# A hybrid decoder trunk on one core: semaphore waits in the scheduler's model, and a lead-in written anew

## The chip, the cores and the metric

The kernel runs on one core of one Trainium2 chip. The metric is the time of one execution on the device in microseconds (us); the median of three runs is given, and beside it one execution that the hardware profiler recorded. Five engines work in parallel, each on its own instruction stream in order: TensorE (PE; its weight loads are listed apart as PEld), VectorE (DVE), ScalarE (ACT), GpSimd (POOL) and SyncE (SP), which issues all transfers here. They wait for each other through semaphores.

## The reference, cut to what matters

Two layers over 1024 positions of 1024 channels in float32, then one RMSNorm. What the change touches is the beginning of the first layer:

```python
def rms_norm(x, g):
    y = x32 * lax.rsqrt(jnp.mean(x32 * x32, axis=-1, keepdims=True) + NORM_EPS)
    return (y * g).astype(x.dtype)

def hybrid_layer(x, c_act, positions, norm_g, w_ada, b_ada, w_in, ...):
    mod = c_act @ w_ada + b_ada
    shift, scale, gate = jnp.split(mod[:, None, :], 3, axis=-1)
    h = rms_norm(x, norm_g) * (1.0 + scale) + shift
    proj = h @ w_in
    ...  # three mixers: windowed pooling, chunked retention, RWKV-7 time mixing
    y = jnp.einsum('btnw,nwd->btnd', branches, w_branch)
    merged = jnp.sum(sigmoid(gate_logits) * y, axis=2)
    return x + gate * (merged @ w_out)

c_act = jax.nn.silu(c)
for l in range(DEPTH):          # DEPTH = 2
    x = hybrid_layer(x, c_act, positions, ...)
return rms_norm(x, final_g)
```

The vector `c_act` has 1024 values and `w_ada` 3072 columns per layer. Nothing can be multiplied by `w_in` before the sum of squares over all channels is known, and slice by slice of channels only when that slice's shift and scale are.

## The kernel before, in words

The activations are held transposed: channels on the 128 partitions, positions along the free dimension. x comes as 16 tiles of 128 x 512: eight slices of channels (kt 0 to 7) in two halves of the sequence (h 0 and 1). Each product of the big projections is made three times in a reduced-precision format (fp32r): an operand is split into a rounded part (`hhi`, or `wh` and the first part of `wbig` for weights) and the rest (`hlo`, `wl`), and hi*hi, hi*lo and lo*hi are added up in PSUM. One such 128x512 matmul is the unit of TensorE's work.

The Python program records all operations first (class `Prog`), and `weave` then sets the order on every engine: it simulates the engines with a table of durations, takes at each step the engine that can start first, and on it the ready operation of the lowest priority number (the recorder's clock, then the order of writing). `give` replays that order; so almost every instruction stands at one line, L500, and is told by its tiles. Waits follow from the data: where an instruction waits for more than one semaphore, the further ones become instructions of their own ahead of it.

The lead-in of layer 0 is written out by hand in the order of `steps`, `sq`, `normed`, `mms` and their like. Its parts:

- `xdma`, `aload`, `wdma`: transfers of x, of the conditioning weights (`wada`, `ringG`) and of the first three weight tiles (`wr`), in that order on SP. At most eight are outstanding.
- `sq`, `sqadd`, `sums`: ACT squares the eight tiles of a half, DVE (and POOL) adds them up, PE sums over the partitions with four 128x1 matmuls against `ones`.
- `rstd`, `rstd_bc`, `rstd_copy`: square root (`rn`), reciprocal, and a broadcast over the partitions by PE (`rbc`), with a copy in SBUF (`rbs`) for POOL.
- `ada`: the conditioning, in groups. Groups 0 to 3 give shift and scale of kt 0 to 3, group 4 of kt 4 and 5, group 5 of kt 6 and 7. Per group DVE takes eight steps "weight tile times c plus the running sum" (`ada_ps`, the last writes `ada_acc`): 256 columns wide in groups 0 to 3, 512 in 4 and 5. Then PE sums over the partitions (`adaps`) and DVE makes `mod` and `acoef`.
- `normed` (x times rbc), `affine` (ACT: `hhi` and x in two passes), `low` (`hlo`), `wsp` (splits the weights: ACT and POOL), `mms`: for one slice and one half nine matmuls, three weight tiles (lora, k, r) by three products. 8 slices x 2 halves x 9 = 144 matmuls.

In the kernel before, `normed` runs on POOL for kt 4 and 5 of both halves and kt 6 and 7 of half 0, and `low` on POOL for kt 1 to 5. After the lead-in a planner (`plan_layer`) feeds the wide matmuls of the projections to PE, and the mixers' small matmuls (the recurrence's `cy`, `ch` above all) are put between them.

Of the kernel before, what the change touches and what calls it, by code (L numbers as in the profile page):

```python
# [9 lines left out]
F32 = mybir.dt.float32  # L10
# [197 lines left out]
class Op:  # L208
    __slots__ = ("eng", "what", "args", "kw", "outs", "ins", "prio", "lane", "pred", "succ", "n", "i",
                 "dur", "occ", "load", "twice", "lock", "est", "start", "end", "left", "table", "acc")  # L210
# [44 lines left out]
SPACE_LAT = {"PE": 54, "DVE": 34, "ACT": 34, "POOL": 70, "SP": 28}  # L255
SETS = {"Sqrt": 1, "Sin": 2, "Tanh": 3, "Exp": 3, "Sigmoid": 3}


class Prog:
# [143 lines left out]
    def weave(self):  # L403
        ops = self.ops
        for o in ops:
            self.cost(o)
            o.est, o.left = 0.0, len(o.pred)
# [6 lines left out]
        landed, table, pe = [0.0] * 8, 0, [0.0, 0.0]  # L414
        order = []
        other = {"DVE": "POOL", "POOL": "DVE"}
        while len(order) < len(ops):
            best = None
            for e, q in ready.items():
                if not q:  # L420
                    continue
                f = free[e]
                if e == "SP":
                    f = max(f, landed[-8])
                elif e == "PE":
                    f = max(pe[0], pe[1] - 107)
                lk = lock[other[e]] - 100 if e in other else 0.0
# [12 lines left out]
            if e == "PE":  # L440
                m = max(pe[1], max(pe[0], o.est) + o.load)
                if o.twice:
                    m += max(o.load, c)
# [10 lines left out]
            order.append(o)  # L454
            for i in o.succ:
                p = ops[i]
                kind = p.pred[o.i]
                if p.eng != e or e == "SP":
                    r = o.end + SPACE_LAT[p.eng]
                elif kind == "d" and e != "PE":  # L460
                    r = o.end + SPACE_LAT[e]
                else:
                    r = s
                p.est = max(p.est, r)
                p.left -= 1
# [38 lines left out]
def trunk_kernel(ctx, tc, xT, cvec, pos, vecs, consts, w_ada, w_all, pool_w, lora_w, out):  # L504
# [1024 lines left out]
    ring = deque()  # L1529
# [31 lines left out]
    def sums(h, *kts):  # L1561
        ssp[h] = acc_ps()
# [88 lines left out]
    def astep(g, nxt=None):  # L1651
        for _ in range(8):
            steps(gs[g], 1)
            if nxt is not None:
                aload(nxt, 1)

# [18 lines left out]
    steps(gs[0], 4)  # L1675
    rstd_bc(0)
    sq(1, 0, 1)
    sqadd(G_, 1, 0, 1)
    steps(gs[0], 4)
    aload(3, 2)  # L1680
    steps(gs[0], 1)
    rstd_copy(0)
    normed(0, 0)
    sq(1, 2, 3)
    sqadd(G_, 1, 2, 3)
    steps(gs[0], 1)
    sq(1, 4, 5)
    sqadd(G_, 1, 4, 5)
    sq(1, 6, 7)
    normed(0, 1)  # L1690
    sqadd(V, 1, 0, 2)
    ss1 = sums(1, 0, 4)
    next(ss1)
    sqadd(V, 1, 6, 7)
    derive(0)
    sqadd(V, 1, 4, 6)
    next(ss1)
    wsp(0, 0)
    affine(0, 0)
    wsp(0, 1, 2)  # L1700
# [4 lines left out]
    steps(gs[1], 3)
    wdma(1, 0, 1, 2)
    aload(4, 6)
    run(ss1)
    acc6[0] = [acc_ps() for _ in range(3)]
    mms(0, 0)  # L1710
    steps(gs[1], 1)
    rstd_bc(1)
    normed(0, 2, 3)
    steps(gs[1], 1)
    normed(0, 4, eng=G_)
    affine(0, 1)
    low(G_, 0, 1)
    steps(gs[2], 2)
    normed(1, 0)
    affine(1, 0)  # L1720
    steps(gs[2], 1)
    normed(1, 1)
    affine(1, 1)
    low(V, 1, 0)
    normed(1, 2, 3)
# [4 lines left out]
    mms(1, 0)  # L1730
    steps(gs[2], 5)
    normed(0, 5, eng=G_)
    steps(gs[2], 1)
    mms(1, 1)
    steps(gs[3], 2)
    steps(gs[2], 1)
    both(2)
    wsp(1, 0)
    normed(1, 4, eng=G_)
    steps(gs[3], 6)  # L1740
    aload(4, 2)
    mms(0, 2)
    steps(gs[3], 1)
    mms(1, 2)
    steps(gs[4], 2)
    steps(gs[3], 1)
    both(3)
    wsp(1, 1, 2)
    normed(1, 5, eng=G_)
    aload(5, 2)  # L1750
    for _ in range(6):
        steps(gs[4], 1)
        aload(5, 1)
    mms(0, 3)
    steps(gs[4], 1)
    mms(1, 3)
    steps(gs[5], 2)
    steps(gs[4], 1)
    both(4)
    both(5)  # L1760
    normed(0, 6, eng=G_)
    normed(0, 7, eng=G_)
    steps(gs[5], 6)
    normed(1, 6, 7, eng=V)
# [327 lines left out]
```

## Time and profile before

| | |
|---|---|
| median of three runs | 2348.25 us (2347.0 to 2361.45) |
| the profiled execution's own time | 2348.31 us |
| its span, first to last instruction | 2346.2 us |
| PE busy | 2302.1 us, 98% |
| DVE, ACT, POOL busy | 1420.2, 859.1, 841.5 us |

The profile lists instructions with start and duration in us from the span's start. A row of a timeline ends, in brackets, with the idle time before it and what ended that; a row of stretches gives the busy time of each engine, then the clock that PE was granted (1.00 or 0.50), the share of the DMA engines and the rate in GB/s. Matmuls are pipelined: a duration overlaps the next one's, and the distance between starts is the cost.

### The profile page before, as it was taken

The numbers are of one execution on the slowest core, as the hardware profiler recorded it, in microseconds if no ns is written. First come the engines' busy times: TensorE is split into PE (matmuls) and PEld (weight loads), VectorE is DVE, ScalarE is ACT, GpSimd is POOL, SyncE is SP. The second block draws the span as 40 slices with busy tenths as digits, with TensorE's granted clock in tenths as the row PEclk, the third lists the DMA queues.
The fourth block names the chain that finished last, engine by engine and source line by source line (L and its number), as shares of the span: only waits on it lengthen the run. The fifth ranks groups of instructions, "written<-read, shape, count | busy, mean of one in ns | idle before, by whom it ended". The sixth has DMA issues, their size and how long they took to land.

```text
span 2346.2 us, 33803 instructions
## 1 busy us (share of the span) xinstructions
PE 2302.1 (98%) x12520; PEld 1905.3 (81%) x12520; DVE 1420.2 (61%) x2802; ACT 859.1 (37%) x1706; POOL 841.5 (36%) x738
## 2 busy tenths in 40 slices
PE   5999999999999999999999999999999999999998
PEld 4888888888888887788888888888788888888888
DVE  7666478467557744468546746855864784412444
ACT  5633342433333333213443334334433423322343
POOL 5222233233242434463442232323323243246541
PEclk9999999999999999999999999999999999999999
DMA  8132112112213315677431211211221131465442
GB/s 280 41 104 77 41 46 87 41 37 69 73 54 91 102 57 175 208 221 235 155 101 52 73 41 41 91 37 39 80 64 38 58 105 53 131 170 157 131 144 81
DMA packets 126516, 227.78 MB, mean 97 GB/s; under 512 B 14352, under 2 KB 17680, under 8 KB 126352
## 3 DMA queue, kind: packets, MB, share of 16 engines
q1 hardware_dynamic: 126352, 225.63, 31.1%
q8 instruction: 98, 1.61, 0.3%
q14 instruction: 66, 0.54, 0.1%
HBM read 176.56 MB, written 49.02 MB: 96 GB/s over the span
## 4 chain that ended last, share of the span: by engine, by line
PE 92%; DVE 4%; DMA 2%; issue 1%; POOL 1%; ACT 1%; SPq 0%; DVEq 0%; ACTq 0%; POOLq 0%
PE acc L500 76%; PE cy L500 4%; PE ch L500 2%; PE g L500 2%; PE m L500 1%; DMA wada<-in_w_ada 1%; PE ro L500 1%; PE bt L500 1%; PE rkv L500 1%; PE rs L500 1%; PE lw L500 1%; DVE ada_acc L500 1%; PE pps L500 0%; SPq L500 0%; DVE ada_ps L500 0%
## 5 line engine op out<-in xcount | busy, mean ns | idle before, releaser
L500 PE MATMUL acc<-hhi,wh 128*128 128x512 f32 x2000 | 806.4, 403 | 0.4 <-DVE r L500 0.4
L500 PE MATMUL acc<-hhi,wl 128*128 128x512 f32 x2000 | 804.7, 402 | 0.0
L500 PE MATMUL acc<-hlo,wh 128*128 128x512 f32 x2000 | 804.4, 402 | 0.0
L500 POOL TENSOR_TENSOR wl<-wr,wh 128x512 fp32r<-128x512 f32 x342 | 455.5, 1332 | 969.2 <-ACT wh L500 938.9
L500 ACT CAST wh<-wr 128x512 fp32r<-128x512 f32 x342 | 212.1, 620 | 618.5 <-PE acc L500 437.2
L500 PEld LDWEIGHTS acc<-hhi,wh 128*128 128x128 f32 x2000 | 377.0, 189 | 66.8 <-issue 1.5
L500 PEld LDWEIGHTS acc<-hhi,wl 128*128 128x128 f32 x2000 | 377.0, 188 | 66.4 <-issue 1.8
L500 PEld LDWEIGHTS acc<-hlo,wh 128*128 128x128 f32 x2000 | 377.1, 189 | 66.0 <-issue 2.2
L500 PE MATMUL acc<-oG,wh 128*128 128x512 f32 x384 | 150.2, 393 | 2.8 <-ACT oG L500 1.5
L500 PE MATMUL acc<-olo,wh 128*128 128x512 f32 x384 | 150.7, 394 | 1.1 <-POOL olo L500 1.0
L500 PE MATMUL acc<-oG,wl 128*128 128x512 f32 x384 | 150.0, 392 | 0.0
L500 ACT COPY xst<-Z 64x64 f32<-64x64 f32 x256 | 62.5, 244 | 168.3 <-DVE Z L500 165.1
L500 DVE SCALAR_TENSOR_TENSOR S<-ch,pc,SP 64x64 f32<-64x64 f32 x224 | 63.3, 283 | 92.0 <-PE ch L500 86.6
L500 DVE COPY xst<-cy 64x64 f32<-64x64 f32 x256 | 55.4, 216 | 86.8 <-PE cy L500 63.1
L500 DVE TENSOR_TENSOR tm<-VB 64x30 f32<-64x30 f32 (+14 forms) x240 | 101.8, 424 | 7.4
L500 DVE TENSOR_TENSOR VB<-VB,tm 64x30 f32<-64x30 f32 (+14 forms) x240 | 99.4, 414 | 7.4
L500 DVE COPY Z<-ch 64x128 f32<-64x128 f32 x128 | 36.0, 281 | 101.4 <-PE ch L500 101.0
L500 PEld LDWEIGHTS acc<-oG,wh 128*128 128x128 f32 x384 | 72.1, 189 | 19.7 <-ACT oG L500 3.2
L500 PEld LDWEIGHTS acc<-olo,wh 128*128 128x128 f32 x384 | 72.6, 189 | 18.3 <-POOL olo L500 3.5
L500 PEld LDWEIGHTS acc<-oG,wl 128*128 128x128 f32 x384 | 72.5, 189 | 14.8
L500 ACT ACTIVATE gsg<-acc 128x512 f32<-128x512 f32 x88 | 52.4, 596 | 84.9 <-PE acc L500 66.5
L500 DVE SCALAR_TENSOR_TENSOR ada_acc<-wada,cact,ada_acc 128x512 f32<-128x512 f32 (+1 forms) x70 | 64.8, 925 | 26.5 <-DMA wada<-in_w_ada 25.6
(269 smaller groups left out, 3688.3 us busy)
## 6 DMA issues: line engine op xcount, KB each, us to landing
wr<-in_w_all SPq DMA_DIRECT2D x364, 256.0 KB, 2.7
gd<-gsg SPq DMA_DIRECT2D x88, 256.0 KB, 2.0
gs<-gd SPq DMA_DIRECT2D x88, 256.0 KB, 2.8
wada<-in_w_ada SPq DMA_DIRECT2D x70, 256.0 KB, 3.6
ol<-od SPq DMA_DIRECT2D x64, 256.0 KB, 2.9
ringG<-in_w_ada SPq DMA_DIRECT2D x26, 256.0 KB, 4.9
x<-in_xT SPq DMA_DIRECT2D x16, 256.0 KB, 5.0
od<-po SPq DMA_DIRECT2D x16, 256.0 KB, 2.1
```

What stands on the lines that cost most here:

```text
L500: f(*[put(x) for x in o.args], **{k: put(x) for k, x in o.kw.items()})
```

## The change

Two things change. First, `weave` gets another model: an operation that waits for new counts of several semaphores starts 140 ns later on PE, and 70 ns after the earlier ones on DVE, ACT and POOL; PE may be chosen 60 instead of 107 ns ahead; and in the first 60 us PE runs at half speed in a window of 3413 ns that follows one with less than 78% of work.

```diff
-                    f = max(pe[0], pe[1] - 107)
+                    f = max(pe[0], pe[1] - 60)
...
-                m = max(pe[1], max(pe[0], o.est) + o.load)
+                k = int(s / WINDOW) if s < WARM_UP else -1
+                slow = 2 if k == 0 or k > 0 and work[k - 1] < 0.78 * WINDOW else 1
+                ld, c = o.load * slow, c * slow
+                m = max(pe[1], max(pe[0], o.est) + ld)
...
-                o.start, o.end = m, m + d
+                o.start, o.end = m, m + d + c - o.occ
...
+                    new = sorted((k for k, (r, n) in p.arr.items() if n > q.get(k, 0)), key=lambda k: SEMS.get(k, 0))
+                    late = max((r for r, n in p.arr.values()), default=0.0)
+                    if len(new) > 1:
+                        if p.eng == "PE":
+                            late += 140
+                        elif p.eng != "SP":
+                            late = max(late, 70 + max(p.arr[k][0] for k in new[:-1]))
+                    p.est = max(p.est, late)
```

Second, the lead-in of layer 0 is written in another order, and two sums move to PE. `ada_both` replaces `ada` for its six groups: in groups 0 to 3 every second weight tile is multiplied on PE (the tile as stationary operand, a column of c moving, 128x1), the others on DVE as before; groups 4 and 5 stay on DVE. The squares of half 0 are no longer added up on DVE: PE sums all eight (32 matmuls instead of 4). Those of half 1 are added in four pairs, all on DVE (16 matmuls instead of 8). `normed` and `low` run on DVE throughout. The second half of x is loaded behind the conditioning weights, and the weight tiles ahead of most of them.

```diff
+    def ada_both(g):
...
+        mine = [i for i in range(2 * n) if i % 2 == 0 and g < 4]
+        kts = [(i, o) for i in range(2 * n) if i not in mine for o in range(per)]
+        for j, (i, o) in enumerate(kts):
...
+                nc.vector.scalar_tensor_tensor(acc if j == len(kts) - 1 else part, w, c, part, op0=ALU.mult, op1=ALU.add)
...
+        todo += [(acc[:, m * P : (m + 1) * P], ones, m) for m in range(n)]
+        for j, (w, c, m) in enumerate(todo):
+            mmul(ps[:, m : m + 1], w, c, start=j == 0, stop=j == len(todo) - 1, skip_group_check=True)
+        ada_end(0, g, ps)
...
-    aload(0, 4)
+    aload(4)
+    wdma(0, 0, 1, 2)
+    aload(10)
     xdma(1, *range(8))
-    wdma(0, 0, 1, 2)
...
-        if kt:
-            sqadd(V, 0, 0, kt)
-    run(sums(0, 0))
+    run(sums(0, *range(8)))
     rstd(0)
...
+    ada_both(0)
...
+    normed(0, 0)
+    affine(0, 0)
...
+    mms(0, 0)
     normed(0, 1)
+    ada_both(1)
...
+    for kt in range(4):
+        normed(1, kt)
+        affine(1, kt)
+        low(V, 1, kt)
+        mms(1, kt)
+    wsp(1, 0, 1, 2)
+    normed(0, 4, 5, 6, 7)
+    normed(1, 4, 5, 6, 7)
+    ada_both(4)
...
+    both(4, V)
+    both(5, V)
     mms(0, 4)
     mms(1, 4)
```

How this moves the instructions is shown at three places. On PE, at the start of the program, before (acc and ssp are PSUM tiles; `fixed` holds `ones`):

```order
L500 MATMUL acc_151<-fixed,sq_103 128x1 x4
L500 MATMUL rbc_179<-cst,rn_164 128x128 x4
L500 MATMUL adaps_192<-fixed,ada_acc_186 128x1 x2
L500 MATMUL acc_242<-fixed,sq_175 128x1 x4
L500 MATMUL acc_253<-hhi_233,wbig_229 128x512 x2
```

and now:

```order
L526 MATMUL ssp_115<-fixed,sq_137 128x1 x4
L526 MATMUL ssp_115<-fixed,sq_143 128x1 x4
L526 MATMUL adaps_202<-cact,ringG_119 128x1 x8
L526 MATMUL adaps_202<-fixed,ada_acc_179 128x1 x2
L526 MATMUL rbc_227<-cst,rn_208 128x128 x4
L526 MATMUL adaps_241<-cact,ringG_119 128x1 x8
L526 MATMUL adaps_241<-fixed,ada_acc_237 128x1
L526 MATMUL acc_265<-hhi_253,wbig_183 128x512 x2
L526 MATMUL acc_269<-hhi_253,wbig_190 128x512 x2
L526 MATMUL acc_276<-hhi_253,wbig_199 128x512 x2
L526 MATMUL adaps_241<-fixed,ada_acc_237 128x1
L526 MATMUL acc_265<-hlo_274,wbig_183 128x512
```

Four matmuls of one sum have become 32 of eight, and behind them stand eight of group 0 (the ring's tiles against c) ahead of the two that sum DVE's part; the second half's sum has gone from this place, and group 1 stands ahead of the first wide matmul.

On SP, behind the constants (`cst`, `vec`), before:

```order
L500 DMA ringG_115<-in_w_ada 128x512 x4
L500 DMA x_130<-in_xT 128x512
L500 DMA x_134<-in_xT 128x512
L500 DMA x_139<-in_xT 128x512
L500 DMA x_142<-in_xT 128x512
L500 DMA x_147<-in_xT 128x512
L500 DMA x_158<-in_xT 128x512
L500 DMA x_166<-in_xT 128x512
L500 DMA x_169<-in_xT 128x512
L500 DMA wr_173<-in_w_all 128x512
```

and now:

```order
L526 DMA ringG_119<-in_w_ada 128x512 x4
L526 DMA wr_135<-in_w_all 128x512
L526 DMA wr_141<-in_w_all 128x512
L526 DMA wr_146<-in_w_all 128x512
L526 DMA ringG_119<-in_w_ada 128x512 x4
L526 DMA wada_173<-in_w_ada 128x512
L526 DMA wada_181<-in_w_ada 128x512
L526 DMA wada_188<-in_w_ada 128x512
L526 DMA wada_196<-in_w_ada 128x512
L526 DMA wada_205<-in_w_ada 128x512
L526 DMA wada_213<-in_w_ada 128x512
L526 DMA x_222<-in_xT 128x512
```

The three weight tiles and ten tiles of conditioning (groups 1, 2 and half of 3) have moved ahead of the eight tiles of the second half, which stood straight behind group 0.

On DVE, the end of group 5, whose `ada_acc` the last conditioning matmuls wait for; before:

```order
L500 SCALAR_TENSOR_TENSOR ada_acc_453<-ringG_115,cact,ada_ps_410 128x512
L500 TENSOR_SCALAR ada_ps_458<-ringG_115,cact 128x512
L500 TENSOR_TENSOR x_166<-x_166,rbs_352 128x512
L500 SCALAR_TENSOR_TENSOR ada_ps_458<-ringG_115,cact,ada_ps_458 128x512 x5
L500 TENSOR_TENSOR x_169<-x_169,rbs_352 128x512
L500 SCALAR_TENSOR_TENSOR ada_ps_458<-ringG_115,cact,ada_ps_458 128x512
L500 SCALAR_TENSOR_TENSOR ada_acc_522<-ringG_115,cact,ada_ps_458 128x512
```

and now, from the last normed tile of half 1 on:

```order
L526 TENSOR_TENSOR x_279<-x_279,rbc_439 128x512
L526 SCALAR_TENSOR_TENSOR ada_ps_398<-wada_375,cact,ada_ps_398 128x512
L526 SCALAR_TENSOR_TENSOR ada_acc_525<-wada_382,cact,ada_ps_398 128x512
L526 TENSOR_SCALAR ada_ps_532<-wada_394,cact 128x512
L526 SCALAR_TENSOR_TENSOR ada_ps_532<-wada_403,cact,ada_ps_532 128x512
L526 SCALAR_TENSOR_TENSOR ada_ps_532<-wada_411,cact,ada_ps_532 128x512
L526 SCALAR_TENSOR_TENSOR ada_ps_532<-wada_421,cact,ada_ps_532 128x512
L526 TENSOR_TENSOR hlo_557<-x_248,hhi_503 128x512
L526 SCALAR_TENSOR_TENSOR ada_ps_532<-ringG_119,cact,ada_ps_532 128x512 x3
L526 TENSOR_TENSOR mod_234<-adaps_575,vec_113 128x4
L526 SCALAR_TENSOR_TENSOR ada_acc_586<-ringG_119,cact,ada_ps_532 128x512
L526 SCALAR_TENSOR_TENSOR acoef_243<-mod_234,vec_113 128x2
```

Before, two normed tiles of half 1 stood between the steps of group 5. Now the last two steps of group 4 and all of group 5 stand behind the last normed tile, with the `hlo` of kt 3, half 1, between them (the six steps of group 4 ahead of them stand in front of half 1's first normed tile); that `hlo` and the `ada_acc` behind it are what PE's next matmuls wait for. On PE four `adaps` matmuls of group 4 and four of group 5 now stand ahead of the first matmul of kt 4; before, those of kt 4 and 5 stood ahead of group 5's.

More of the change, by code (lines that the diff above doesn't have):

```diff
@@ L209 @@
     __slots__ = ("eng", "what", "args", "kw", "outs", "ins", "prio", "lane", "pred", "succ", "n", "i",
-                 "dur", "occ", "load", "twice", "lock", "est", "start", "end", "left", "table", "acc")
+                 "dur", "occ", "load", "twice", "lock", "est", "start", "end", "left", "table", "acc", "arr", "seq")
 class Engine:
@@ L255 @@
 SPACE_LAT = {"PE": 54, "DVE": 34, "ACT": 34, "POOL": 70, "SP": 28}
+WARM_UP, WINDOW = 60000.0, 3413.0
+SEMS = {"DVE": 1, "PE": 2, "ACT": 3, "POOL": 4}
 SETS = {"Sqrt": 1, "Sin": 2, "Tanh": 3, "Exp": 3, "Sigmoid": 3}
@@ L406, in weave @@
             self.cost(o)
-            o.est, o.left = 0.0, len(o.pred)
+            o.est, o.left, o.arr = 0.0, len(o.pred), {}
+        count = {}
+        seen = {e: {} for e in SPACE_LAT}
         free = {e: 0.0 for e in SPACE_LAT}
@@ L414, in weave @@
         landed, table, pe = [0.0] * 8, 0, [0.0, 0.0]
+        work = [0.0] * (int(WARM_UP / WINDOW) + 2)
         order = []
@@ L454, in weave @@
             order.append(o)
+            src = f"SP{len(landed) % 8}" if e == "SP" else e
+            o.seq = count[src] = count.get(src, 0) + 1
+            for k, (r, n) in o.arr.items():
+                seen[e][k] = max(seen[e].get(k, 0), n)
             for i in o.succ:
                 p = ops[i]
-                kind = p.pred[o.i]
                 if p.eng != e or e == "SP":
                     r = o.end + SPACE_LAT[p.eng]
-                elif kind == "d" and e != "PE":
+                elif p.pred[o.i] == "d" and e != "PE":
                     r = o.end + SPACE_LAT[e]
@@ L1561, in sums @@
     def sums(h, *kts):
-        ssp[h] = acc_ps()
+        ssp[h] = ps_c.tile([P, HF], F32, tag="ch", name=nm("ssp"), bufs=1)
         for kt in kts:
@@ L1649, in both @@
             low(eng or G_, h, kt)
[L1651 to L1655, printed above, removed]
     cond_act()
@@ L1674, in trunk_kernel @@
     rstd(0)
-    steps(gs[0], 4)
     rstd_bc(0)
[L1677 to L1682, printed above, removed]
-    normed(0, 0)
[L1684 to L1689, printed above, removed]
-    normed(0, 1)
[L1691 to L1700, printed above, removed]
@@ L1701, in trunk_kernel @@
-    steps(gs[1], 2)
-    low(V, 0, 0)
-    steps(gs[1], 3)
-    rstd(1)
[L1705 to L1711, printed above, removed]
-    rstd_bc(1)
[L1713 to L1725, printed above, removed]
+    derive(0)
@@ new lines, in trunk_kernel @@
+    ada_both(0)
+    aload(4)
+    acc6[0] = [acc_ps() for _ in range(3)]
+    normed(0, 0)
+    affine(0, 0)
+    wsp(0, 0)
+    low(V, 0, 0)
+    wsp(0, 1, 2)
+    wdma(1, 0, 1, 2)
+    mms(0, 0)
+    normed(0, 1)
+    ada_both(1)
+    aload(4)
+    affine(0, 1)
+    low(V, 0, 1)
+    mms(0, 1)
+    normed(0, 2, 3)
+    for kt in range(8):
+        sq(1, kt)
+        if kt % 2:
+            sqadd(V, 1, kt - 1, kt)
+    ada_both(2)
+    aload(4)
+    affine(0, 2)
+    low(V, 0, 2)
+    mms(0, 2)
@@ L1726, in trunk_kernel @@
+    run(sums(1, 0, 2, 4, 6))
+    ada_both(3)
+    aload(4)
+    affine(0, 3)
+    low(V, 0, 3)
+    mms(0, 3)
+    rstd(1)
+    rstd_bc(1)
     rstd_copy(1)
-    low(G_, 1, 1)
-    mms(0, 1)
     acc6[1] = [ps_c.tile([P, HF], F32, tag=t, name=nm("acc"), bufs=n) for t, n in (("ch", 1), ("cy", 2), ("cy", 2))]
[L1730 to L1764, printed above, removed]
+    for kt in range(4):
[3 more added lines that the diff above has]
+        mms(1, kt)
@@ L1765, in trunk_kernel @@
+    wsp(1, 0, 1, 2)
+    normed(0, 4, 5, 6, 7)
+    normed(1, 4, 5, 6, 7)
+    ada_both(4)
+    aload(8)
+    both(4, V)
+    both(5, V)
     mms(0, 4)
     mms(1, 4)
-    steps(gs[5], 1)
     mms(0, 5)
     mms(1, 5)
-    steps(gs[5], 1)
+    ada_both(5)
     both(6, V)
```

48 lines of the change are left out of this document (36 added, 12 removed).

## The prediction

> **What bounds the kernel now.** I read the page first: how long TensorE (PE) is busy, and which chain ended last.
>
> ```profile
> span 2346.2 us, 33803 instructions
> PE 2302.1 (98%) x12520; PEld 1905.3 (81%) x12520; DVE 1420.2 (61%) x2802; ACT 859.1 (37%) x1706; POOL 841.5 (36%) x738
> PE 92%; DVE 4%; DMA 2%; issue 1%; POOL 1%; ACT 1%; SPq 0%; DVEq 0%; ACTq 0%; POOLq 0%
> ```
>
> PE is idle for 2346.2 - 2302.1 = 44.1 us in all, and 92% of the chain is PE. What one can win is therefore idle time of PE, or time at half clock. The busy time by stretches says where the idle time lies. Columns: length, then busy us and instructions of PE, PEld, DVE, ACT, POOL, then granted clock, DMA share, GB/s.
>
> ```profile
> 10.00:20.00 10.00, 4.59 (x20) 4.42 (x20) 7.97 (x21) 6.38 (x11) 2.92 (x3) 1.00 1.05 389
> 20.00:30.00 10.00, 5.13 (x16) 3.76 (x16) 9.58 (x17) 4.06 (x7) 9.94 (x9) 1.00 1.05 387
> 40.00:61.42 21.42, 15.30 (x51) 12.09 (x52) 18.48 (x31) 11.79 (x17) 16.55 (x14) 0.76 0.57 185
> 61.42:81.43 20.01, 20.01 (x97) 16.77 (x95) 6.61 (x17) 14.68 (x22) 6.17 (x7) 1.00 0.14 40
> 81.43:925.40 843.97, 843.14 (x4800) 695.68 (x4799) 551.67 (x1170) 319.01 (x667) 264.87 (x240) 1.00 0.23 71
> 925.40:946.00 20.60, 16.00 (x64) 10.88 (x62) 12.54 (x17) 5.48 (x10) 11.32 (x9) 0.92 0.83 268
> 946.00:2335.00 1389.00, 1386.43 (x7426) 1151.63 (x7427) 799.39 (x1504) 484.55 (x954) 523.25 (x444) 1.00 0.34 104
> 2335.00:2346.20 11.20, 3.04 (x20) 2.60 (x18) 3.24 (x9) 1.14 (x3) 1.42 (x2) 0.62 0.28 94
> ```
>
> From 61.42 on PE is full. Between 81.43 and 2335 it idles 0.83 + 4.60 + 2.57 = 8.0 us, of which 4.6 stand at the layer boundary, and in the last 11 us another 8.2; the remaining 27.9 us lie in the lead-in. So the lead-in decides: the 144 first matmuls (three weight tiles, two halves of the sequence, eight slices kt, three products each) end at 81.43, and what makes this moment earlier comes straight off the end. What holds PE back until 61.42 is shown by PE's timeline (start, duration, instruction, count, idle before and its releaser).
>
> ```profile
> 11.74 1.87 PE L500 MATMUL acc<-fixed,sq 128*128 128x1 f32 x8 [11.74 <-DVE sq L500]
> 24.41 1.63 PE L500 MATMUL acc<-hhi,wbig 128*128 128x512 f32 x3
> 52.54 0.56 PE L500 MATMUL adaps<-fixed,ada_acc 128*128 128x1 f32 x2 [3.39 <-DVE ada_acc L500]
> 68.24 0.94 PE L500 MATMUL adaps<-fixed,ada_acc 128*128 128x1 f32 x8
> 77.35 1.52 PE L500 MATMUL acc<-hhi,wbig 128*128 128x512 f32 x6
> 79.39 1.52 PE L500 MATMUL acc<-hhi,wbig 128*128 128x512 f32 x6
> 81.43 0.39 PE L500 MATMUL acc<-hhi,wbig 128*128 128x512 f32 x1
> ```
>
> PE waits for DVE: for the sums of squares, then for the conditioning (ada_acc). From 77.35 to 79.39 stand nine matmuls, so one takes 0.227 us. Four of the program's 128x1 matmuls stand in the trace as eight passes: 1.87 us early, 0.94 us late, so 0.47 or 0.235 us for one. That factor of two is the clock. It can be read window by window:
>
> ```profile
> 40.62:44.03 3.41, 1.02 (x5) 0.49 (x3) 3.31 (x6) 2.19 (x4) 3.41 (x4) 1.00 0.38 98
> 44.03:47.45 3.42, 3.08 (x7) 2.48 (x8) 3.28 (x6) 1.24 (x2) 3.42 (x3) 0.50 0.72 210
> 47.45:50.86 3.41, 1.70 (x10) 1.35 (x8) 2.52 (x6) 0.00 (x0) 1.74 (x2) 1.00 0.96 315
> 50.86:54.27 3.41, 1.73 (x5) 1.56 (x6) 3.38 (x7) 2.50 (x4) 0.83 (x1) 0.50 0.98 354
> 54.27:57.69 3.42, 3.42 (x9) 2.65 (x9) 3.28 (x6) 3.35 (x5) 3.07 (x3) 0.50 0.52 181
> 57.69:61.10 3.41, 3.41 (x16) 2.77 (x16) 2.11 (x3) 1.89 (x4) 3.15 (x4) 1.00 0.01 2
> ```
>
> A window in which PE was busy 1.02, 1.70 or 1.73 of 3.41 us is followed by one at 0.50, a window of 3.08 or 3.42 by one at 1.00. (Before 37 us the records say 1.00, but the 1.87 us above show half clock.) The windows also show DVE full, 3.3 of 3.4 us, while PE is not: in the lead-in DVE is the pacemaker.
>
> **The change part by part.** Durations come from these rows: DVE by groups (busy, mean ns) and single rows, then ACT.
>
> ```profile
> L500 DVE SCALAR_TENSOR_TENSOR ada_ps<-ringG,cact,ada_ps 128x512 f32<-128x512 f32 x12 | 9.1, 754 | 0.3
> L500 DVE SCALAR_TENSOR_TENSOR ada_ps<-ringG,cact,ada_ps 128x256 f32<-128x256 f32 x15 | 7.3, 487 | 0.3
> L500 DVE TENSOR_TENSOR x<-x,rbc 128x512 f32<-128x512 f32 x8 | 5.1, 684 | 4.5 <-PE rbc L500 3.3 <-ACT rbs L500 1.2
> L500 DVE TENSOR_TENSOR hlo<-x,hhi x6: 684/693/1755, 32.2 to 76.7; 128x512 fp32r<-128x512 f32 x6
> 10.99 0.69 DVE L500 TENSOR_TENSOR sq<-sq,sq 128x512 f32<-128x512 f32 x1
> 59.09 0.75 DVE L500 SCALAR_TENSOR_TENSOR ada_acc<-ringG,cact,ada_ps 128x512 f32<-128x512 f32 x1
> L500 ACT ACTIVATE x<-x,mod,acoef 128x512 f32<-128x512 f32 x8 | 6.5, 815 | 0.3
> L500 ACT CAST wbig<-wr 128x512 fp32r<-128x512 f32 x8 | 4.8, 610 | 1.2 <-DMA wr<-in_w_all 1.2
> L500 ACT ACT_TABLE_LOAD x3 | 3.8, 1283 | 0.8 <-PEq L2081 0.7
> L500 ACT ACTIVATE rn<-acc,fixed 128x4 f32<-128x4 f32 x2 | 0.5, 264 | 9.9 <-PE acc L500 9.9
> 3.95 1.38 ACT L500 ACTIVATE sq<-x 128x512 f32<-128x512 f32 x2 [0.21 <-DMA x<-in_xT]
> 7.92 2.78 ACT L500 ACTIVATE sq<-x 128x512 f32<-128x512 f32 x4 [0.35 <-DMA x<-in_xT]
> 5.45 5.44 DMA vec<-in_vecs
> ```
>
> (a) The transfers. vec lands at 5.45 + 5.44 = 10.89 us, and then 389 GB/s move a 256 KB tile in 0.67 us. In the new order the four tiles of conditioning group 0 land by 13.6, the three weight tiles by 15.6, group 1 by 18.3, groups 2 and half of 3 by 22.3, the second half of x by 27.7 (before, it stood straight behind group 0). The second half's squares are added on DVE at about 26 to 31, so its later landing is just covered; with the cover gone it costs what it is late by.
>
> (b) The first squares. The seven additions on DVE (7 x 0.69) go, 28 further 128x1 matmuls come. ACT ends the first square at 3.95 + 0.69 and the last at 7.92 + 2.78 = 10.70. On PE the eight groups of four start at 4.7: three at 1.87 us, then, after a full window, five at 0.94, so 15.0 against 11.74 + 1.87 = 13.6. Yet ACT is queued to cast the weight tiles (last landing 15.6, + 0.6) and to load a table (1.28) before rn (0.27): 17.8. DVE takes the reciprocal and must still wait for group 1's last tile (18.3), then do its two steps, mod and acoef. **The first normed x starts at 19.65, against 16.96 before: 2.7 us lost.**
>
> (c) The conditioning of groups 0 to 3: each has four steps of 0.51 us on DVE instead of eight, and eight 128x1 matmuls on PE. Since group 1 now stands ahead of the first x, 24 such steps behind it become 8: 8.2 us less. But DVE now does what POOL did: behind the first x and ahead of group 5's end stand 16 normed x instead of 10, 8 hlo instead of 2, 4 additions instead of 3: 6 x 0.64 + 7 x 0.69 = 8.7 us more. In work DVE wins nothing there; it can only win in waits.
>
> (d) So DVE from the first normed x to the end of group 5: 16 x at 5.1 / 8 = 0.64, 10.2 us; 8 hlo x 0.69 = 5.5; 4 additions x 0.69 = 2.8; 8 steps of 256 columns x 0.51 (0.487 and the distance to the next) = 4.1; 16 of 512 x 0.785 (0.754, likewise) = 12.6; mod, acoef and a reciprocal 1.3. Sum 36.5. Waits: 0.5 for PE's first adaps, 0.7 for ACT's copy of rbc, which stands ahead of the second half's x, about 0.8 for affine results, and 1.0 for steps that find POOL at work (the 1755 ns of the hlo row against its median of 693; fewer such meetings than before, as POOL has fewer tiles to do). 19.65 + 36.5 + 3.0 = **59.1, against 59.09 + 0.75 = 59.84.** DVE is hardly earlier; what changes is what PE has done by then.
>
> (e) PE at that moment: 72 of the 144 matmuls (kt 0 to 3 of both halves) stand ahead of group 5's four adaps, which wait for that last ada_acc. Before, 20.01 us of work were left at 61.42. Now 59.1 + 0.94 + 72 x 0.227 = 76.4, and as PE idles ahead of those adaps, I take half a window at half clock, 0.85 us (the last hlo of kt 3 stands 3.3 us ahead of DVE's end, at 55.8; three wide matmuls and group 4's adaps later PE is done at 57.4 and waits 1.7 us): **77.3 against 81.43, 4.1 us won.** ACT makes a slice's two affines in 2 x 0.82 us, PE uses it in 2.04, so ACT hides there; so do the hlo (0.69).
>
> (f) The scheduler's waits. Weight loads of the recurrence wait as well, partly under a running matmul:
>
> ```profile
> PEld cy L500 <- ACT y L500: 13.8, 52, 0.6
> ```
>
> PE instructions that wait for two semaphores or more are 183 before and 185 after; behind the lead-in about a hundred of 10,800 PE rows stand one or two places elsewhere, and the number of long matmuls between the steps of the recurrence is the same in all but a few cases. Bounds: to win, the 8.0 us of visible idle time and these 13.8 at most; to lose, as much again if every shift goes the wrong way. I take 0, the value nearest to the unchanged order.
>
> The sum: 2348.31 us is the profiled execution's own time (2.1 around its span), next to the median of 2348.25. 2348.3 - 4.1 = **2344 us**.
>
> [...]
>
> **The rivals.**
> *Half clock makes PE the bound (slower than before).* From 19.65 to 59.1 PE has 72 x 0.227 + 50 x 0.235 + 2 x 0.94 = 30 us of work at full clock in 39.5 us. If over 32% of it runs at half clock, PE is later than DVE, and every adaps that DVE waits for shifts. For it: three of the six windows shown ran at 0.50. With 60% PE needs 48 us, 8.5 late: 2352.5. Against it: each full window brought 1.00 back, so a late PE cures itself. Chance 0.17.
> *More is won.* DVE's waits and its meetings with POOL vanish (3 us), PE loses no window (0.85), and the small shifts take half of the 8.0 us of idle time: 2344 - 3 - 0.85 - 4 = 2336. For it: the lead-in is written anew, engine by engine. Against it: steps in a row still pass from DVE to ACT to DVE to PE, and the order behind 81 us is nearly the same. Chance 0.2.
> *Partial work keeps the clock up*, so that PE loses no window ahead of group 5's adaps: 2343. Three windows (1.02, 1.70 and 1.73 us of work, 0.50 after each) speak against it. Chance 0.05. [...]
> *It doesn't do what it says.* The double waits stay, and POOL, which splits five weight tiles at 50 to 58 us, meets hlo and additions four more times at 1 us each: 2348, no change. Chance 0.1.
> *The transfers.* If the second half of x lands 3 us later than (a) counts, DVE waits for its squares: 2347, a part of the forecast's own range.
>
> **How the numbers follow.** The forecast (2340 to 2347, with the last case) has 0.48, the others together 0.52. A measurement of this kernel tells about 1% from no change, 23 us: no case reaches it, and most of PE's 27.9 us of idle lead-in would have to go. I leave 0.03 on each side for what I have not seen, and 0.94 within. The range goes from 2335 to 2352: it takes in the second rival and about half of the first.
>
> **What would show it.** The first normed x near 19.7; the first wide matmul near 21 instead of 24.4; PE idle near 57 to 59 ahead of adaps; the first wide matmul behind the lead-in at 77 instead of 81.4; from there to 2335 the same idle time within 3 us. I am wrong in DVE's sum if its last ada_acc ends beyond 63 or ahead of 56, in the clock if most windows from 20 to 58 stand at 0.50, and in (f) if the stretch behind the lead-in is shorter or longer by over 5 us.

## The result and the profile after

The changed kernel takes 2364.32 us (median of 20 runs, 2352.27 to 2375.65), the kernel before 2351.97 us (median of 20 on the same chip, 2346.25 to 2361.45). The ratio is 1.0054, 95% interval 1.0040 to 1.0067: 12.7 us more (0.54% of the time before), where 4 us less were forecast. It is still within 1% of before; the range (2335 to 2352) did not hold it, and the sign was wrong.

The profiled execution took 2358.84 us (before 2348.31). The page:

```profile
span 2357.1 us, 34029 instructions
PE 2332.2 (99%) x12656; PEld 1934.7 (82%) x12656; DVE 1418.1 (60%) x2796; ACT 857.6 (36%) x1705; POOL 823.5 (35%) x719
PE 93%; DVE 3%; DMA 2%; issue 1%; POOL 0%; ACT 0%; SPq 0%; DVEq 0%; POOLq 0%; ACTq 0%
```

PE is busier than before (30 us more) and idles 24.9 us instead of 44.1, and yet the span is 10.9 us longer. So the idle time was indeed won back, and something was paid for it. The stretches of the changed kernel (columns as before):

```profile
10.00:20.00 10.00, 10.00 (x49) 10.00 (x49) 3.95 (x12) 4.33 (x7) 3.72 (x3) 1.00 1.05 381
20.00:30.00 10.00, 10.00 (x44) 9.61 (x45) 4.71 (x10) 2.67 (x4) 0.11 (x1) 1.00 1.05 386
40.00:61.42 21.42, 19.31 (x67) 16.50 (x68) 14.35 (x25) 11.84 (x18) 2.85 (x3) 0.55 0.42 129
87.63:932.00 844.37, 844.12 (x4794) 696.09 (x4793) 553.06 (x1168) 318.42 (x665) 263.32 (x239) 1.00 0.22 71
932.00:957.00 25.00, 19.28 (x72) 14.13 (x71) 14.58 (x19) 6.07 (x10) 12.84 (x10) 0.86 0.74 236
957.00:2346.00 1389.00, 1386.19 (x7424) 1150.46 (x7423) 799.56 (x1504) 483.70 (x954) 530.19 (x444) 1.00 0.33 104
```

From 10 to 30 us PE is full where before it was half idle, and now it is DVE that waits: it is busy for 3.95 and 4.71 of 10 us, before for 7.97 and 9.58. The chain of work that ended last runs on PE alone from 4.6 to 49.6 us; its pieces (start, us, what) begin so:

```profile
4.60 13.81 PE ssp L526 x64
18.42 4.27 PE adaps L526 x20
22.68 1.92 PE rbc L526 x8
24.60 3.63 PE adaps L526 x18
28.23 2.77 PE acc L526 x6
```

64 passes in 13.81 us are 0.216 us each. That is the price at half clock: where this profile's records give 0.50, ten such passes take 2.13 us (39.14 to 41.27), and where they give 1.00, twenty take 2.15 (36.38 to 38.53), 0.21 and 0.11 us each. So PE ran 13.8 us on end at half clock. In PE's timeline the lead-in's last part and the first wide matmul behind it (start, us, instruction):

```profile
28.09 2.91 PE L526 MATMUL acc<-hhi,wbig 128*128 128x512 f32 x6
68.70 1.08 PE L526 MATMUL adaps<-fixed,ada_acc 128*128 128x1 f32 x8 [1.19 <-DVE acoef L526]
69.64 2.91 PE L526 MATMUL acc<-hhi,wbig 128*128 128x512 f32 x6
87.63 0.39 PE L526 MATMUL acc<-hhi,wbig 128*128 128x512 f32 x1
```

The lead-in ends at 87.63 instead of 81.43: 6.2 us lost. Behind it PE idles 0.25 + 5.72 + 2.81 = 8.8 us up to 2346, against 8.0 before; two more windows of 3.41 us at a recorded clock of 0.50 (at 619, 940 and 950 us, against one at 931.5 before) cost, as an estimate from that clock, up to half their length, 1.7 us, each. 6.2 + 0.8 + 3.4 = 10.4 us, about the 10.5 us between the two profiled executions.

In the table below the end of the lead-in is 81.43 plus the shift of the same later instruction against before (ACT's 16th `wh` cast); for the changed kernel this gives 87.6, as the timeline does. Both times in the table come from one profiled execution of each kernel, the ratios from 7 to 20 runs of each, against before on the same chip. One profiled end can mislead: three executions of the changed kernel, below, end their lead-in at 87.6, 92.3 and 95.3.

### The profile page after: what moved, and what is told of

The parts are those of the page before. It is cut to its first block, busy times and chain, and to the rows that moved or that the text cites. A ratio compares the mean times of both kernels' runs of the same rounds, so it can differ in the third digit from the quotient of the medians.

```text
span 2357.1 us, 34029 instructions
## 1 busy us (share of the span) xinstructions
PE 2332.2 (99%) x12656; PEld 1934.7 (82%) x12656; DVE 1418.1 (60%) x2796; ACT 857.6 (36%) x1705; POOL 823.5 (35%) x719
## 4 chain that ended last, share of the span: by engine, by line
PE 93%; DVE 3%; DMA 2%; issue 1%; POOL 0%; ACT 0%; SPq 0%; DVEq 0%; POOLq 0%; ACTq 0%
PE acc L526 75%; PE cy L526 4%; PE ch L526 2%; PE g L526 2%; PE m L526 1%; PE ro L526 1%; DMA wada<-in_w_ada 1%; PE adaps L526 1%; PE ssp L526 1%; DVE ada_acc L526 1%; PE rkv L526 1%; PE bt L526 1%; PE rs L526 1%; PE lw L526 1%; PE pps L526 0%
## 5 line engine op out<-in xcount | busy, mean ns | idle before, releaser
L526 POOL TENSOR_TENSOR wl<-wr,wh 128x512 fp32r<-128x512 f32 x342 | 463.1, 1354 | 974.3 <-ACT wh L526 948.9
```

What stands on the lines that cost most here:

```text
L526: f(*[put(x) for x in o.args], **{k: put(x) for k, x in o.kw.items()})
```

## The experiments

Four explanations were put to the test. Theory C: the clock follows the columns that stream through PE and not its busy time, so a PE filled with 128x1 matmuls stays at half clock and becomes the bound. Rival D: DVE is the bound, since it does POOL's share. Rival M: the new scheduler model costs. Rival B: the clock follows the busy share.

| kernel | first normed x | end of lead-in | ratio to before, 95% |
|---|---|---|---|
| before | 17.0 | 81.4 | |
| changed | 24.6 | 87.6 | 1.0054, 1.0040 to 1.0067 |
| model_only | 18.5 | 79.1 | 1.0003, 0.9985 to 1.0021 |
| leadin_only | 24.7 | 92.2 | 1.0024, 1.0008 to 1.0041 |
| squares_dve | 19.4 | 90.0 | 1.0062, 1.0039 to 1.0085 |
| cond_dve | 23.0 | 82.7 | 1.0022, 1.0004 to 1.0039 |
| both_dve | 18.4 | 78.0 | 1.0009, 0.9989 to 1.0029 |
| pool_back | 19.9 | 86.2 | 1.0038, 1.0020 to 1.0056 |
| ones128 | 20.0 | 82.3 | 1.0014, 0.9997 to 1.0031 |
| ones128_both | 19.0 | 77.3 | 0.9980, 0.9965 to 0.9995 |
| stream_half | 18.6 | 79.2 | 1.0008, 0.9992 to 1.0024 |
| w_half | 19.3 | 72.7 | 0.9977, 0.9961 to 0.9994 |
| w_half_old | 17.3 | 73.6 | 0.9976, 0.9958 to 0.9994 |
| w_all | 18.9 | 85.5 | 1.0014, 0.9997 to 1.0030 |

### The model, or the lead-in

model_only is the old lead-in under the new `weave`; leadin_only the new lead-in under the old one (the two halves of each file exchanged at `trunk_kernel`).

```diff
-                    f = max(pe[0], pe[1] - 107)
+                    f = max(pe[0], pe[1] - 60)
...
+                        if p.eng == "PE":
+                            late += 140
```

This is model_only against before, with the other lines of `weave` in the change's diff; leadin_only takes the same lines back from the changed kernel.

> Only the new scheduler model, with the lead-in as it was before. Theory C (clock): the loss is in the new lead-in, where TensorE is kept busy by 128x1 matmuls that do not bring the clock up; the model alone moves few instructions, so the lead-in ends at 81 +- 1.5 us and the time is within 3 us of before. Rival M (model): the waits that the model adds cost the 4 to 6 us that the changed kernel loses behind the lead-in (it is 6.2 us late at 87.6 us and 11 us late at the end); then this kernel is 4 to 6 us slower than before, with the loss between 580 and 1220 us.

> The changed lead-in with the scheduler model of before. Theory C: the loss is in the lead-in and not in the model, so the lead-in ends at 85 to 91 and the time is 8 to 14 us above before. Rival M (the model, made for the lead-in but wrong on the clock, puts the single-column matmuls into bad places): without it the loss is under 5 us.

The model alone changes nothing that can be measured (1.0003), so M falls as the whole cause. leadin_only has the late lead-in (92.2 in its profile) but loses only 5.7 us by its ratio (1.9 to 9.6), less than the 8 to 14 expected. So the new lead-in loses time without the model; the other 7 of the 12.7 us appear only with both together, and whether the model makes this one lead-in worse is left open (the two intervals just touch, 1.0041 and 1.0040). Under the lead-in w_half no difference between the models shows (below).

### Undoing one part of the lead-in, or both

```diff
     for kt in range(8):            # squares_dve, both_dve
         sq(0, kt)
-    run(sums(0, *range(8)))
+        if kt:
+            sqadd(V, 0, 0, kt)
+    run(sums(0, 0))
...
-        mine = [i for i in range(2 * n) if i % 2 == 0 and g < 4]
+        mine = []                  # cond_dve, both_dve
```

> The changed kernel with one part undone: the first half's squares are added up on VectorE again (7 additions, 4 matmuls of 128x1 instead of 32). Theory C: the 32 matmuls at half clock (13.8 us) and the conditioning behind them push the first normed x from 17.0 to 24.6 us; with 4 of them the sum ends near 13.6, group 0's conditioning takes its 4.3 us at half clock, and the first normed x starts at 20.4 +- 0.7; the lead-in ends near 84 instead of 87.6, and the time is 3 to 5 us less than the changed kernel's. Rival D (VectorE is the bound since it does GpSimd's share): 4.8 us of additions more on VectorE, so the lead-in ends at 87.6 or later and the time is the same or up to 4 us more.

> The changed kernel with the other part undone: the conditioning of groups 0 to 3 wholly on VectorE (16 more steps of 0.51 us, 32 fewer 128x1 matmuls on TensorE). Theory C: the half clock between 38.8 and 59.3 us goes in part, because its windows were filled with 128x1 matmuls; rbc stands behind 2 instead of 10 conditioning matmuls, so the first normed x starts at 21.5 +- 1; VectorE has about 12 us of idle time between 24 and 68 us that takes the 8.2 us up; the lead-in ends 1 to 5 us earlier than 87.6. Rival D: 8.2 us more on VectorE, the lead-in ends at 90 or later and the time is 3 to 8 us more than the changed kernel's.

> The changed kernel with both parts undone: squares and conditioning on VectorE, while normed and low stay on VectorE, and the transfers and the order stay as changed. Theory C: the first normed x back near 17 to 18 us and hardly a full window at half clock behind 30 us, but VectorE now carries 13 us more than in the changed kernel and becomes the bound (its last ada_acc near 68 to 70); the lead-in ends at 85 to 88. Rival D: the sum of VectorE's work alone decides, so the lead-in ends 13 us later than the changed kernel's, near 100.

With both parts back on DVE the loss is gone (1.0009, lead-in 78.0), although DVE has 13 us more to do: rival D, which put the end near 100, falls. Theory C missed here as well, since it took DVE for the new bound and put the end at 85 to 88. With the conditioning alone back, more than half of the loss is gone (1.0022); the first normed x came at 23.0, later than the 20.5 to 22.5 expected. The squares alone back did not bring the 3 to 5 us of theory C: the first normed x came at 19.4, 1 us ahead of what was expected, and then the lead-in ended later, at 90.0, as rival D had it for this run. Two lines of its PE timeline, one from the middle and one from 52.7 us on:

```profile
35.37 3.55 PE L526 MATMUL ssp<-fixed,sq 128*128 128x1 f32 x16
52.78 1.64 PE L526 MATMUL acc<-hhi,wbig 128*128 128x512 f32 x6
```

0.22 us a pass at 35 us is half clock, and no pass at full clock comes before 52.7, though PE is full (3.41 of 3.41 us in 39.06:42.47 and 42.47:45.88). In the changed kernel's profile the clock had come up at 32.0. What decides that could not be read from these four.

### The clock: the same matmuls with more columns

In the records of the changed kernel the granted clock changes at 31.99, 38.82, 59.30, 69.54 and 72.95 us, in those of before at 37.21, 44.03, 47.45, 50.86 and 57.69: the neighbours among these lie one, two, three or six times 3.41 us apart. One such step is called a window here, and the question is which windows were followed by which clock.

ones128 changes one operand of the first sum: the same 32 matmuls with the same weights, against 128 columns of ones instead of one (the square root reads the first column of each result). ones128 does so for half 0, ones128_both for both halves.

```diff
-                    ssp[h][:, m : m + 1], sqs[h, kt][:, m * P : (m + 1) * P], ones,
+                    ssp[h][:, m * P : (m + 1) * P], sqs[h, kt][:, m * P : (m + 1) * P], ones128,
```

> The changed kernel with one operand wider: in the first half's sum the moving operand is 128 columns of ones instead of one (the same 32 matmuls, the same weights, the same order; only the first column of each result is used). Theory C, refined: the clock follows what is streamed through TensorE, not how long TensorE counts as busy; windows of the changed kernel with under 3000 streamed columns of 3.41 us are followed by half clock although they are full of 128x1 matmuls. Here a full window at half clock holds some 13 passes of 128 columns, 1700 columns (3400 if a float32 pass counts twice). If these suffice, the sum ends by 14 instead of 18.4 us, although each matmul has more to do, and the first normed x starts 3 to 5 us earlier than 24.6; if not, the sum ends at 19.5 +- 0.7 (passes of 0.257 instead of 0.235 us) and the count of a float32 pass is one. Rival B (the busy share sets the clock): a full window is a full window, nothing changes but the 1.4 us of longer passes, and the half clock in full windows needs another cause (for example a fixed time from the start until the clock comes up).

PE's timeline and windows of ones128:

```profile
4.75 8.77 PE L526 MATMUL ssp<-ones,sq 128*128 128x128 f32 x64 [4.75 <-ACT sq L526]
13.36 1.84 PE L526 MATMUL adaps<-cact,ringG 128*128 128x1 f32 x16
4.25:7.66 3.41, 2.91 (x14) 2.94 (x15) 0.00 (x0) 2.17 (x4) 0.00 (x0) 1.00 0.97 337
7.66:11.08 3.42, 3.42 (x32) 3.42 (x32) 0.46 (x4) 2.59 (x5) 0.00 (x0) 1.00 1.03 387
17.90:21.32 3.42, 3.42 (x17) 3.42 (x17) 2.39 (x7) 0.60 (x1) 0.50 (x2) 0.50 1.05 386
```

Matmuls with 128 times the columns end 5 us earlier (13.5 instead of 18.4 us): some 13 passes in the 2.91 us of the first window (0.22 us each), some 30 in the next (0.11 us). (The last line shows half clock again from 17.9 us, behind a window with 1.17 us of work.) The time falls by 9 us against the changed kernel (1.0014 against 1.0054). Rival B, by which a full window is a full window, falls. And the first window bears on the count: it held 1,676 columns (13.1 passes of 128) and passes at 0.11 us followed, where a window of after_look2 (27.43:30.84, below) held 3,080, six wide matmuls, and passes at 0.21 us followed. With a float32 column counted twice the first has more than the second (3352); this factor is an estimate, worked out from these two windows and not measured by itself.

With that count (columns of every pass, those of float32 matmuls doubled, spread from a matmul's start to the next one's or to its own end) the windows of the first 100 us of the 17 profiles of this case, some 375 whose next clock is on record, divide without an exception outside a narrow band: every window below 3,070 columns was followed by half clock, every one above 3,110 by full clock, and of five between 3,072 and 3,102 three were followed by full and two by half. Most of them lie far from the band. At full clock 2,630 columns were followed by half (47.45:50.86 of before) and 3,690 by full (31.99:35.40 of the changed kernel); at half clock 3,102 were followed by half (62.28:65.69 of ones128) and 3,095 by full (50.90:54.31 of after_look, below). Windows full of wide matmuls held 7,710 columns at full clock (62.71:66.12 of the changed kernel, 0.227 us a matmul) and 4,142 at half (54.27:57.69 of before, 0.427 us); so the band lies at 40% of the one and 75% of the other. Some windows of the changed kernel:

```profile
14.92:18.34 3.42, 3.42 (x18) 3.42 (x17) 1.11 (x3) 2.75 (x4) 3.11 (x3) 1.00 1.05 392
28.58:31.99 3.41, 3.41 (x10) 2.74 (x9) 0.89 (x5) 0.08 (x1) 0.00 (x0) 1.00 1.05 386
38.82:42.23 3.41, 3.41 (x18) 3.41 (x17) 2.88 (x8) 2.22 (x5) 0.00 (x0) 0.50 0.22 78
45.64:49.06 3.42, 3.42 (x14) 2.99 (x12) 0.00 (x0) 0.00 (x0) 0.00 (x0) 0.50 0.59 182
55.88:59.30 3.42, 3.42 (x10) 2.65 (x9) 2.87 (x6) 3.35 (x6) 0.00 (x0) 0.50 0.00 0
59.30:62.71 3.41, 3.41 (x16) 2.79 (x15) 3.30 (x6) 2.77 (x5) 1.57 (x2) 1.00 0.00 0
```

All six are full. Counted from their matmuls, the first and third hold 32 columns (16 passes), the fourth 2,100 (four wide matmuls beside 128x1): half clock follows. The second holds 3,590 (seven wide ones), the fifth 4,130: full clock follows. (Ahead of the first change of clock, here at 32.0, the records say 1.00; the passes of 0.22 us show half.) squares_dve fits this: its windows between 22 and 49 us held 2,730 columns at most, and behind the window with 4,130 the wide matmuls went from 0.43 to 0.23 us at 52.7.

One window ahead of the first change of clock widens the band. w_all (below) begins with the same 64 wide passes as ones128, but its windows lie otherwise: 4.09 to 7.50 us held 3,177 columns by this count, and half clock went on for one window more, which shows in the time of the 64 passes (8.77 us in ones128):

```profile
4.73 10.33 PE L526 MATMUL ssp<-ones,sq 128*128 128x128 f32 x64 [4.73 <-ACT sq L526]
```

The changed kernel twice more under the profiler, and the kernel before once more, with no edit:

> The changed kernel again, one look. Theory C with a free-running clock window: the lead-in's end depends on where the 3.41 us windows fall, since a window near 3100 columns goes either way; it lies between 84 and 94 us (87.6 in the first profile), at 90 +- 3 on average, and its distance to the end of the kernel varies by up to 12 us through later half-clock windows. If the lead-in were fixed, 87.6 +- 0.5.

> As after_look: another execution of the changed kernel, lead-in's end between 84 and 94 us if the windows' phase decides, 87.6 +- 0.5 if not.

> The kernel before again, one look: its lead-in has few single-column matmuls, so its end varies less, 81.4 +- 2 us; what differs from the first profile's 2348.3 us comes from half-clock windows behind the lead-in (time minus the clock's loss was constant within 2 us over its runs).

The lead-in of the changed kernel ended at 92.3 and 95.3 us (2365.7 and 2363.0 us in all), that of before at 80.8 (2349.55). In the second of these executions of the changed kernel the windows lay 1.15 us earlier against the work (from 27.43 instead of 28.58), and the one that holds the first wide matmuls got 3,080 columns instead of 3,590; half clock went on until 65 us, as this line of its timeline shows beside the window:

```profile
27.43:30.84 3.41, 3.41 (x11) 2.83 (x11) 1.34 (x3) 0.67 (x2) 0.11 (x1) 1.00 1.05 385
40.23 4.26 PE L526 MATMUL ssp<-fixed,sq 128*128 128x1 f32 x20
62.33 1.49 PE L526 MATMUL acc<-hlo,wbig 128*128 128x512 f32 x3
```

So the changed lead-in hangs on where the windows fall, and the first profile was the lucky one of the three. The 20 timed runs fit this: their time less what the recorded clock cost (one minus the mean granted clock, times the span) is 2335 to 2341 us in ten, the first profiled one among them, and 2346 to 2355 in the other ten, where the two later executions lie as well (2349 and 2354). Half clock ahead of the first recorded change is not in that cost, so the second ten may be those whose clock came up late; their lead-ins were not traced. The mean of the three ends is 91.7, 10.3 us behind 81.4; that leaves some 2 us of the 12.7 for what lies behind, within the spread of half-clock windows there.

### Giving tiles back to POOL

```diff
-    normed(0, 4, 5, 6, 7)
-    normed(1, 4, 5, 6, 7)
+    normed(0, 4, 5, 6, 7, eng=G_)
+    normed(1, 4, 5, eng=G_)
+    normed(1, 6, 7)
```

> The kernel with squares and conditioning on VectorE (both_dve; lead-in ends at 78.0 us) with normed of kt 4 and 5 and of kt 6 and 7 of half 0, and hlo of kt 1 to 5, given back to GpSimd as before. Theory D (VectorE's share of GpSimd's work costs): 8.7 us less on VectorE, the lead-in ends 3 to 6 us earlier, 72 to 75. Theory C (these tiles were cover, not a cost): GpSimd needs 1.3 to 1.8 us a tile and slows VectorE's steps beside it, so the lead-in ends at 78 to 81 and the time is that of both_dve within 3 us.

Both expectations missed: 86.2. The timelines show one reason that has nothing to do with the tiles' price; the first two lines are from DVE and PE here, the third from PE in both_dve:

```profile
26.13 0.22 DVE L526 SCALAR_TENSOR_TENSOR acoef<-mod,vec 128x1 f32<-128x1 f32 x2
27.45 2.91 PE L526 MATMUL acc<-hhi,wbig 128*128 128x512 f32 x6
20.75 2.93 PE L526 MATMUL acc<-hhi,wbig 128*128 128x512 f32 x6 [2.40 <-ACT hhi L526]
```

The order came out with kt 0's `acoef` at 26.1, behind group 2's steps, and the first wide matmul at 27.45 instead of 20.75. The run shows that giving the tiles back helps nothing in this order; what they cost by themselves it does not tell.

### Keeping the sums and the conditioning on PE, with columns

stream_half turns PE's half of the conditioning round: c is the stationary operand and 256 columns of the weight tile move. The rest is squares_dve, but for one line that gives the scheduler a duration for such a matmul.

```diff
-        todo = [(aw[g][i][:, o * W_ + m * P : o * W_ + (m + 1) * P], cact[:, i * per + o : i * per + o + 1], m)
-                for i in mine for o in range(per) for m in range(n)]
+                col = cact[:, i * per + o : i * per + o + 1].to_broadcast([P, P])
+                mmul(row, col, aw[g][i][:, o * W_ : (o + 1) * W_], start=j == 0, stop=j == len(mo_) - 1)
...
+            nc.scalar.copy(rows, row)
+            todo += [(rows[:, m * P : (m + 1) * P], ident[:, 0:1], m) for m in range(n)]
```

> The kernel with squares on VectorE (squares_dve; lead-in ends at 90.0 us, TensorE at half clock without a break until 52.7 us) with TensorE's half of the conditioning turned round: c (broadcast to 128 columns) is the stationary operand and 256 columns of the weight tile move, four 128x256 matmuls instead of eight 128x1, then a copy on ACT and two 128x1 matmuls. VectorE has the same work. Theory C: the streamed columns lift the clock from about 25 us on, most windows from 30 to 55 us run at 1.00, and the lead-in ends at 78 to 84; the time is 6 to 12 us less than that of squares_dve. Rival B (busy share): as many or more busy microseconds, the same clock, so the lead-in ends at 89 to 92. Rival D (VectorE's work is the bound): no change either, 90 +- 1.

> ones128 with the second half's sum done likewise (16 matmuls against 128 columns of ones instead of one). In ones128 the clock fell to half at 31.6 to 38.4 us, behind the windows that these 16 matmuls fill with single columns. Theory C: those windows now stream over 3100 columns, no half clock between 28 and 58 us, and the lead-in ends 2 to 5 us ahead of that of ones128 (82.2), at 77 to 80. Rival B (busy share): unchanged, 82 +- 1.

> ones128_both, and TensorE's half of the conditioning of groups 0 to 3 turned round as in stream_half (256 columns of the weight tile move past c). Theory C: no window between 8 and 55 us that is full and yet at half clock; the lead-in ends at 73 to 77, earlier than both ones128_both and stream_half (79.2), and the time is 3 to 7 us below that of before. Rival D (VectorE's steps for groups 4 and 5 are the bound at about 55 to 60 us): the lead-in ends at 77 to 79, as in both.

> w_half with groups 0 to 3 conditioned on TensorE alone (eight 128x256 matmuls of 0.48 us per group, no step on VectorE). VectorE has 8 us less ahead of groups 4 and 5. Theory C: TensorE has 7.7 us more to stream, at full clock; if VectorE's end decides, the lead-in ends 3 to 6 us ahead of w_half's, and the time is 6 to 11 us below before; if TensorE's own work decides, it is that of w_half +- 2 us.

> w_half (lead-in ends at 72.6 us, time 2349.5) with the scheduler model of before. Rival M, in what is left of it (the new model costs 3 to 5 us behind the lead-in, through more windows of small matmuls at half clock): the time is 3 to 6 us below w_half's, 2344 to 2347. Theory C alone (what is lost behind the lead-in is chance, the same for both models): the same time within 2.5 us if the lead-in ends within 2 us of 72.6.

stream_half ends its lead-in at 79.2, 10.8 us ahead of squares_dve with the same work on DVE, and is 0.54% faster; from its timeline:

```profile
18.72 1.97 PE L526 MATMUL adarow<-ringG,cact 128*128 128x256 f32 x8
20.88 1.65 PE L526 MATMUL acc<-hhi,wbig 128*128 128x512 f32 x6 [0.19 <-ACT hhi L526]
```

Eight passes in 1.97 us, and the first wide matmuls at full clock at 20.9 us. ones128_both (the second half's sum wide too) ends at 77.3, w_half (ones128_both and stream_half's conditioning) at 72.7, with one window at 0.50 behind 8 us (18.26:21.68). A window of it that the second half's sum fills, in which the changed kernel lost its clock:

```profile
28.50:31.92 3.42, 3.42 (x30) 3.24 (x28) 3.24 (x7) 1.77 (x5) 0.10 (x1) 1.00 1.05 387
29.28 2.39 PE L526 MATMUL ssp<-ones,sq 128*128 128x128 f32 x20
```

w_half beats before by 0.23% (0.06 to 0.39%) and the changed kernel by 0.77% (1.0054 to 0.9977): the change's own idea, with columns in its matmuls. w_half_old is the same under the old model, 0.9976. The two ratios agree, so nothing of rival M shows here; but each is known to some 0.17% only, and the 3 us that it asked for at the least are 0.13%.

w_all differs from w_half in the split and in the PSUM tile of the row:

```diff
-        mine = [i for i in range(2 * n) if i % 2 == 0 and g < 4]
+        mine = list(range(2 * n)) if g < 4 else []
...
+            row = mx("adarow")[:, 0:W_]
```

It missed: 85.5. Its clock came up one window later than that of ones128 (above), and the PSUM buffers chosen for it stood in the way; group 4's first step on DVE waits for a copy of group 3's row, where its buffer comes free:

```profile
44.35 0.75 DVE L526 TENSOR_SCALAR ada_ps<-ringG,cact 128x512 f32<-128x512 f32 x1 [3.42 <-ACT adarow L526]
```

So it does not tell whether the other half of the conditioning belongs on PE. stream_all, the same split on stream_half, gave no time.

## Why the prediction was wrong, point by point

- **(a), transfers: right.** ACT's squares of the second half wait for no transfer; its 2.0 us of waits for x all lie in the first half.

```profile
ACT sq L526 <- DMA x<-in_xT: 2.0, 3, 1.5
```

- **(b), the first squares: the step that failed.** It put five of eight groups of the sum at 0.94 us "after a full window", as if any window that PE fills brought the clock up. Here a window full of 128x1 matmuls held 32 columns and did not (14.92:18.34 above, and 0.21 us a pass behind it): the groups took 1.73 us to the last, and the sum ended at 18.4 instead of 15.0. Then group 0's twenty passes on PE, 4.27 us in the chain above, stand ahead of rbc; (b) had put nothing for them. The first normed x came at 24.64, not 19.65:

```profile
24.64 2.48 DVE L526 TENSOR_TENSOR x<-x,rbc 128x512 f32<-128x512 f32 x4 [1.30 <-PE rbc L526]
```

- **(c), DVE's work: right** in what it counts; 13 us of it put back (both_dve) cost nothing.
- **(d), DVE's end: work right, waits wrong.** From the first normed x to the end of group 5 it took 43.9 us (24.64 to 68.56) instead of 36.5 + 3.0; DVE was busy for 33.4 of them. DVE's waits for PE's adaps and its last `ada_acc`:

```profile
DVE mod L526 <- PE adaps L526: 11.1, 4, 4.7
67.81 0.75 DVE L526 SCALAR_TENSOR_TENSOR ada_acc<-ringG,cact,ada_ps 128x512 f32<-128x512 f32 x1
```

  The 0.5 us that were put for "PE's first adaps" became 11.1 us for four groups, 3.4 of them ahead of the first x and 7.7 behind it: the same half clock (0.50 from 38.82 to 59.30), since PE at that price was later than DVE. "DVE hardly earlier", 59.1, became 68.6, beyond the 63 that was to show the sum wrong.
- **(e), the last 72 matmuls: right in form.** PE idled 1.19 us ahead of group 5's adaps (1.7 forecast), lost one window there at a clock of 0.50 (69.54:72.95), and needed 18.0 us for the 72 (87.63 - 69.64; 72 x 0.227 = 16.3 at full clock).
- **(f), the model: right as far as shown.** 8.8 against 8.0 us of idle time behind the lead-in; model_only 1.0003. What the model does to the new lead-in was not in (f), and leadin_only leaves it open.
- **The baseline.** 2348.3 us stood for a kernel whose median over 20 runs is 2352.0. 3.7 of the 20.3 us between forecast and median are this.
- **The rival** that half clock makes PE the bound is what happened. It had 0.17 and 2352.5 us. Its price was too low, since it had only a later PE and not a later first normed x, and the reason against it was false: "each full window brought 1.00 back, so a late PE cures itself" came from windows full of wide matmuls. The windows in the prediction's own list already fit the count: the 3.08 us of work in 44.03:47.45, nearly all wide matmuls and 3,510 columns, were followed by 1.00, the 1.70 us of the next window, 2,630 columns, by 0.50. But they could not tell columns from busy time, because no window in it was full of 128x1 matmuls. In the changed kernel PE was busy without a gap from 4.60 to 28 us, nearly seven windows, and a pass still took 0.21 us (adaps, 24.39 to 27.67).

## What to carry to other kernels

Work that moved to TensorE to fill its idle time cost its clock here: a full window of 1,580 columns was followed by 0.50 (35.40:38.82 of the changed kernel), and one of 32 too (38.82:42.23). So count the columns of each window of the profile, not its busy time. Sums over partitions and matrix-vector products can be turned so that many columns move past one stationary operand, or be given idle columns; here that was worth 0.4% (ones128) to 0.8% (w_half) against the changed kernel. Where a window comes near the band of 3,070 to 3,110 columns that these profiles showed, one profile may be a lucky phase: three executions of the changed kernel ended their lead-in at 87.6, 92.3 and 95.3 us, so look at two or three before a difference of 5 us is put down to a change.

## What the runs showed of the hardware

- In the 17 profiles the clock of the next window went with the columns of a window of 3.41 us, float32 columns counted twice: below 3,070 half clock followed, above 3,110 full clock, but for one of 3,177 ahead of the first recorded change (4.09:7.50 of w_all). At half clock 3,080 (27.43:30.84 of after_look2), 3,102 and 3,177 were followed by half and 3,095 by full; at full clock 2,630 were followed by half and 3,690 by full. These are counts of this kernel's variants, and nothing else was tried.
- More work was faster: 64 passes took 13.81 us with one column (the changed kernel) and 8.77 us with 128 (ones128).
- The spread of the kernel before went with such windows as well: over 35 of its runs the time less the recorded clock's cost stayed between 2333 and 2341 us, while that cost went from 9.4 us in the fastest to 28.4 us in the slowest.
